# Low parts taken from GpSimd in the expert stages, and an earlier first chunk in two projections

## The chip, the cores and the metric

One core of one Trainium2 chip. The metric is the device time of one execution, in microseconds; the kernel before was timed in 3 runs.

## The reference

Two residual layers and a final RMSNorm over 1024 positions of 1024 values. Each layer normalises, projects, mixes tokens, projects out, and then runs an expert-choice mixture of experts. What matters here is the input projection and the experts:

```python
h = rmsnorm(x, norm_mix[i])
proj = h @ w_in                      # even: 1024 x 2816, odd: 1024 x 1184
...
# experts: 16, each takes its 128 best tokens
gates, idx = lax.top_k(aff.transpose(0, 2, 1), cap)
xs = h[idx]
g = xs @ w_gate                      # 1024 x 512 for each expert
u = xs @ w_up                        # 1024 x 512
y = (silu(g) * u) @ w_down           # 512 x 1024
out[idx] += y * gates
```

Everything is float32. The kernel keeps that precision by splitting each operand into a high part (rounded to the matmul's format) and a low part (the rest), and by adding three products: high by high, high by low, low by high.

## The kernel before, in words

The program is one order of work, written out by hand, for one core: even projection, dilated attention with a gMLP, output projection and routing, 16 experts, odd projection, dense attention, output projection and routing, 16 experts, final norm. Each engine runs its own instructions in that order, and waits only where data or a buffer is missing.

**The weight stream (class Stream, L163).** All weights of the program are one list of pieces of 128x1024 values (512 KB). `load` issues the next pieces on SyncE's queue (L202, L204) while there is a free slot for raw pieces; `conv` makes the high part on ScalarE (L225, or L235 with a gain) and then the low part, raw minus high, on VectorE (L232, or L236), and gives the raw slot back. With `pool=True` L232 goes to GpSimd (POOL) instead. The converted pieces lie in eight buffer pairs in the expert stages.

**The experts (out_moe).** For expert e the order on TensorE is: four pieces of "up" (`gate_up(e, "u", q)`, 6 matmuls of 128x512 each), with the first half of the next expert's tokens transposed after the second piece (`xsT`, L588); then the other half of these transposes, the 8 small matmuls of `index(e + 3)` (L572), four pieces of "gate" of expert e + 1, with the 4 transposes of `hT(e)` (L628) after the second; and four pieces of "down" (L644). VectorE makes `sg` = up times silu(gate) (L622), which `hT` transposes, and besides it the low parts `xl` and `tl` of the transposed operands (L149), the one-hot matrix of a later expert (L565) and the indices (L574, L576). GpSimd gathers the tokens (L578) and scatters the result (L659). After each piece `ahead(j)` (L593) converts the piece 7 places further on and issues loads. One piece in 12 has its low part made by POOL; that is the second "down" piece of expert e, which comes up after the third "up" piece of that expert, one for each of experts 0 to 14 in each layer. The output projection of layer 0 also gives low parts to POOL (four), in a call of its own.

**The projections (even_proj, odd_proj, class NormProj).** The tokens come in eight chunks of 128. `trans(c)` transposes chunk c on TensorE (8 transposes, L790), splits it in two halves (L148 on ScalarE, L149 on VectorE) and sums its squares (L793); `stat` turns these into 1/rms (13 tiny VectorE instructions in the even layer); `mm(c, j, n)` multiplies the chunk by four pieces, 8 steps of 3 matmuls (L259 to L261), two steps to a piece. In both projections chunks 0 and 1 are transposed before the first `mm`, and chunk c + 2 after `mm` of chunk c. In the even layer the queue of loads is: x chunk 0, weight pieces 0 and 1, x chunk 1, pieces 2 and 3, x chunks 2 and 3, further pieces as slots come free. In the odd layer the first four pieces are converted before the chunks of x can be read, since these wait for the last scatter of layer 0.

Of the kernel before, what the change touches and what calls it, by code (L numbers as in the profile page):

```python
# [257 lines left out]
def mm3(nc, out, ah, al, bh, bl, first, last):  # L258
    nc.tensor.matmul(out, ah, bh, start=first, stop=False)  # L259
    nc.tensor.matmul(out, ah, bl, start=False, stop=False)  # L260
    nc.tensor.matmul(out, al, bh, start=False, stop=last)  # L261
# [23 lines left out]
def out_moe(k, layer, stream, at, cva, n_a, n_early, n_late, mix, xload, xres, hd, out=None):  # L285
# [10 lines left out]
    with ExitStack() as ctx:  # L296
        ctx.enter_context(tc.manual_schedule())
        cvc = ctx.enter_context(tc.tile_pool(name=f"cvc{layer}", bufs=1, reuse_waits="tile")) if n_a < 4 else None
        base = at["out"]
# [6 lines left out]
        with lp, tk:  # L306
# [22 lines left out]
            g = k.gain(p2, i["norm_ffn"][layer], "gffn")  # L329
# [102 lines left out]
            for c in range(1, NCH):  # L432
# [3 lines left out]
                for s in range(16):  # L436
                    n, kk = divmod(s, 8)
# [30 lines left out]
            c = NCH - 1  # L468
# [56 lines left out]
            n = 64  # L525
# [62 lines left out]
                nc.tensor.transpose(pt[:, kk], d["xs"][:, c0:c0 + 128], k.ident)  # L588
            k.split(d["xh", q], d["xl", q], pt)

        AHEAD, EVERY = 7, 12

        def ahead(j):  # L593

            n = min(j + 1 + AHEAD, at["end"])
            while stream.n_conv < n:
                stream.conv(stream.n_conv + 1, pool=(stream.n_conv - at["g", 0]) % EVERY == 1, load=False)
            stream.load()

        def gate_up(e, nm, q):  # L600
# [166 lines left out]
class NormProj:  # L767
# [27 lines left out]
    def stat(self, c0, c1):  # L795
        self.k.rsqrt(self.p2, self.rstd[:, c0:c1], self.ss[:, c0:c1], EPS, 1.0 / DM, f"rs{c1 - c0}")

    def mm(self, c, j, n):

        nc = self.k.nc  # L800
        pt = self.pp.tile([128, 512], F32, name="pp")
        sl = slice(c * 128, (c + 1) * 128)
        for kk in range(NCH):
            bh, bl = self.stream.part(j + kk // 2, kk % 2, n)
            mm3(nc, pt[:, 0:n], self.hT[:, 0, kk, sl], self.hT[:, 1, kk, sl], bh, bl, kk == 0, kk == 7)
        return pt
# [27 lines left out]
def even_proj(k, stream, x_in, qk, vd, gd, first):  # L834

    tc, nc, i = k.tc, k.nc, k.i
    with ExitStack() as ctx:
        ctx.enter_context(tc.manual_schedule())  # L840
        p1 = ctx.enter_context(tc.tile_pool(name="ep1", bufs=1, reuse_waits="tile"))
        p2 = ctx.enter_context(tc.tile_pool(name="ep2", bufs=2, reuse_waits="tile"))
        cv = ctx.enter_context(tc.tile_pool(name="ecv", bufs=6, reuse_waits="tile"))
        ps = ctx.enter_context(tc.tile_pool(name="eps", bufs=2, space=PSUM, reuse_waits="tile"))
        pp = ctx.enter_context(tc.tile_pool(name="epp", bufs=3, space=PSUM, reuse_waits="tile"))
        gps = ctx.enter_context(tc.tile_pool(name="gps", bufs=2, space=PSUM, reuse_waits="tile"))
        stream.into((cv, 6))
        P = NormProj(k, stream, p1, p2, pp, ps)
        rq = p1.tile([128, NCH], F32, name="rq")
        z = p1.tile([128, NCH, 512], F32, name="z")  # L850
        von = p1.tile([128, 2, 8, 66], F32, name="von")
        k.consts(p1, "rac", "ras", nc.gpsimd)
        ra_c = k.c("rac").rearrange("p (c f) -> p c f", c=8)
        ra_s = k.c("ras").rearrange("p (c f) -> p c f", c=8)

        def stat(c0, c1):
            P.stat(c0, c1)
            nc.vector.tensor_scalar(rq[:, c0:c1], P.rstd[:, c0:c1], 0.125, None, op0=ALU.mult)

        def evac(kind, cols, c, pt):  # L860
            sl = slice(c * 128, (c + 1) * 128)
            if kind == "z":
                nc.scalar.activation(z[:, c], pt, AF.Gelu_apprx_tanh, scale=P.rstd[:, c:c + 1])
                return
            if kind == "v":
                (c0, n), = cols
                nh = n // 64
                h0 = (c0 - 1536) // 64
                ov = von[:, c % 2, 0:nh]
                nc.scalar.activation(ov[:, :, 0:64], pt[:, 0:n].rearrange("p (h d) -> p h d", d=64), AF.Copy,  # L870
                                     scale=P.rstd[:, c:c + 1])
                nc.gpsimd.dma_start(vd[sl, h0:h0 + nh], ov)
                return
            o = p2.tile([128, 512], F32, name="po", bufs=3)
            a = 0
            for c0, n in cols:
                nc.scalar.activation(o[:, a:a + n], pt[:, a:a + n], AF.Copy,
                                     scale=(rq if c0 < 768 else P.rstd)[:, c:c + 1])
                a += n
            ov = o.rearrange("p (h d) -> p h d", d=64)[:, :, 0:16]  # L880
            rope(nc, p2, ov, ov, ra_c[:, c, None, :].to_broadcast([128, 8, 8]),
                 ra_s[:, c, None, :].to_broadcast([128, 8, 8]), 8, "r")
            dst, a = (qk[1], 0) if len(cols) == 2 else (qk[0], 0 if kind == "q" else 512)
            nc.gpsimd.dma_start(dst[sl, a:a + 512], o)

        bg = []
        xs, gx = ExitStack(), ExitStack()
        P.xp = xs.enter_context(tc.tile_pool(name="exp", bufs=4, reuse_waits="tile"))

        def load(c):  # L890
            P.load(c, x_in[c * 128:(c + 1) * 128], nc.sync)
        load(0)
        stream.load(2)
        load(1)
        stream.load(4)
        load(2)
        load(3)
        P.trans(0)
        stream.conv(2)
        stat(0, 1)  # L900
        stream.conv(4)
        P.trans(1)
        stat(1, 2)
        nc.vector.memset(von[:, :, :, 64:66], 1.0)
        j = 0
        for gi, (kind, cols) in enumerate(EVEN_GROUPS):
            last = gi + 1 == len(EVEN_GROUPS)
            for c in range(NCH):
                if gi + 2 == len(EVEN_GROUPS) and c == 5:
                    gx.close()  # L910
                    bg = first(ps, cv)
                pt = P.mm(c, j, sum(n for _, n in cols))
                if gi == 0:
                    if c + 2 < NCH:
                        P.trans(c + 2)
                        stat(c + 2, c + 3)
                        if c + 4 < NCH:
                            load(c + 4)
                    if c == 2:
                        k.rest()  # L920
                    if c == 5:
                        xs.close()
                        gp = gx.enter_context(tc.tile_pool(name="gp1", bufs=1, reuse_waits="tile"))
                        bg = gmlp(k, z, gd, gp, gps)
                evac(kind, cols, c, pt)
                if not last and c in (1, 3, 6, 7):
                    if c == 7:
                        stream.drop(j, 4)
                    stream.conv(j + 4 + (1, 3, 6, 7).index(c) + 1)
                if gi and bg:  # L930
                    bg.pop(0)()
            j += 4
        stream.drop(j - 4, 4)
# [475 lines left out]
def odd_proj(k, stream, base, xin, cT, kp, krs, cdr, qd, kd, vdd, heads):  # L1409
# [4 lines left out]
    with ExitStack() as ctx:  # L1414
# [9 lines left out]
        P = NormProj(k, stream, p1, p2, pp, ps)  # L1424
# [3 lines left out]
        def load(c):  # L1428
            P.load(c, xin[c * 128:(c + 1) * 128], nc.sync if c < 3 else nc.scalar, DM if c else 512)
# [28 lines left out]
        def trans_c(c):  # L1458
            o = oc.pop(c)
            tp = ps.tile([128, 4, 128], F32, name="pt")  # L1460
            for j in range(3):
                nc.tensor.transpose(tp[:, j], o[:, j * 128:(j + 1) * 128], k.ident)
            sl = slice(c * 128, (c + 1) * 128)
            k.split(cT[:, 0, :, sl], cT[:, 1, :, sl], tp[:, 0:3])

        P.trans(0)
        P.stat(0, 1)
        P.trans(1)
        P.stat(1, 2)
        for c in range(NCH):  # L1470
            if c == 2:
                k.consts(p0, "rcc", "rds", nc.gpsimd)
            pt = P.mm(c, base, 416)
            if c + 2 < NCH:
                P.trans(c + 2)
                P.stat(c + 2, c + 3)
            if c + 3 < NCH:
                load(c + 3)
            if c > 1 and c % 2:
                for a in (c - 3, c - 2):  # L1480
                    trans_c(a)
            if c == 7:
                stream.conv(base + 8)
            evac_c(c, pt)
            if c % 2:
                norm_c(c - 1, c + 1)
            if c in (1, 3):
                stream.conv(base + {1: 5, 3: 6}[c])
# [67 lines left out]
        for part, j, n in (("q", base + 4, 512), ("k", base + 8, 256)):  # L1556
            tables(part)
            for c in range(NCH):
                pt = pts.pop(0) if pts else P.mm(c, j, n)
# [58 lines left out]
        def transpose4(dst, src):  # L1618
# [6 lines left out]
            else:  # L1625
                H.late.append(lambda: nc.scalar.activation(dst, cat(pt), AF.Copy))
        first = H.prep(0, transpose4)
        between = {(1, 0): [lambda: H.kr(0, None)], (1, 1): [lambda: H.kr(1, transpose4)] + first[2], (2, 0): first[3], (2, 1): first[4],
                   (3, 0): first[7], (3, 1): first[8]}
# [446 lines left out]
```

## Time and profile before

| what | value |
| --- | --- |
| runs | 2043.83, 2044.11, 2040.78 us; median 2043.83 |
| profiled execution | 2040.48 us, span 2038.7 us |
| TensorE busy | 1867.7 us (92%), granted clock 0.970 in the mean |
| VectorE busy | 1507.7 us (74%) |
| ScalarE busy | 1245.2 us (61%) |
| POOL busy | 504.1 us (25%) |
| low parts on VectorE, L232 into lo, raw from the ring | 243, mean 1416 ns |
| transfers | 384.78 MB, mean 189 GB/s |

Busy shares are means over stages with different limits, so the sections below go by stage. The expert stages run from about 655 to 962 us and from about 1690 to 2000 us of the span; the even projection starts with the span, the odd one at about 970 us. In the views, times are microseconds from the start of the span, a bracket holds the idle time ahead of an instruction and what ended it, and a group's time runs from the start of its first instruction to the end of its last.

### The profile page before, as it was taken

The page shows a single profiled execution, that of the slowest core. Times are in us where ns is not written, and L with a number is a line of the kernel's source. Part 1 is how long each engine was busy: PE and PEld are TensorE (multiplying, and loading weights), DVE is VectorE, ACT ScalarE, POOL GpSimd, SP SyncE. Part 2 cuts the span into 40 slices and gives each one's busy share as a digit, 9 for nine tenths or more (in the row PEclk, how much of TensorE's full clock was granted, in tenths as well). Part 3 has the DMA queues.
Part 4 walks back from the last instruction along what each step waited for, and adds up shares of the span by engine and source line. Part 5 has one row for each costly group of instructions (what it writes and reads, how often), then busy time and mean ns, then how long its engine had stood idle before and what let it go on. Part 6 is the DMA issues. An engine that isn't in the chain of part 4 may idle for free. (4 is left out here: it accounts for less than half of the span.)

```text
span 2038.7 us, 29998 instructions
## 1 busy us (share of the span) xinstructions
PE 1867.7 (92%) x10350; PEld 1563.4 (77%) x10350; DVE 1507.7 (74%) x3092; ACT 1245.2 (61%) x2020; POOL 504.1 (25%) x426
## 2 busy tenths in 40 slices
PE   8999999998995999998998799999998968999993
PEld 6888899997883777776887688888886846777772
DVE  5431246776557999997776688889995569999994
ACT  5322257775324777776634688889883326877783
POOL 0010100002102443541002243322212014444334
PEclk9999999999997999999899999999999979999996
DMA  6232355542555999994326554424115848999955
GB/s 228 71 104 78 128 138 136 128 122 85 207 208 181 378 384 373 373 385 95 124 78 209 95 75 87 69 45 54 37 30 163 305 169 311 384 372 387 375 183 196
DMA packets 214171, 384.78 MB, mean 189 GB/s; under 512 B 71937, under 2 KB 122881, under 8 KB 214018
## 3 DMA queue, kind: packets, MB, share of 16 engines
q1 hardware_dynamic: 190082, 303.43, 45.6%
q0 software_dynamic: 21200, 73.13, 12.0%
q10 hardware_dynamic: 2736, 6.29, 0.9%
q8 instruction: 82, 1.34, 0.3%
q14 instruction: 71, 0.58, 0.1%
HBM read 309.13 MB, written 66.32 MB: 184 GB/s over the span
## 5 line engine op out<-in xcount | busy, mean ns | idle before, releaser
L232 DVE TENSOR_TENSOR lo<-raw,hi 128x1024 fp32r<-128x1024 f32 x243 | 334.0, 1416 | 12.2 <-ACT hi L225 12.2
L225 ACT ACTIVATE hi<-raw 128x1024 fp32r<-128x1024 f32 x269 | 275.1, 1055 | 15.3 <-PE py L644 12.1
L259 PE MATMUL pp<-hi,hT 128*128 128x512 f32 (+2 forms) x576 | 213.2, 370 | 0.0
L260 PE MATMUL pp<-lo,hT 128*128 128x512 f32 (+2 forms) x576 | 211.6, 367 | 0.1
L261 PE MATMUL pp<-hi,hT 128*128 128x512 f32 (+2 forms) x576 | 211.2, 367 | 0.0
L1866 DVE TENSOR_REDUCE nm<-css 128x1 f32<-128x1024 f32 x128 | 156.0, 1219 | 41.3 <-PE css L1860 40.8
L149 DVE TENSOR_TENSOR PT<-cpt,PT 128x512 fp32r<-128x512 f32 x256 | 163.1, 678 | 4.3 <-ACT PT L148 1.9
L148 ACT ACTIVATE PT<-cpt 128x512 fp32r<-128x512 f32 x256 | 139.6, 597 | 40.4 <-PE cpt L1884 38.7
L1860 PE MATMUL css<-kT,qT 128*128 128x512 f32 x512 | 151.7, 398 | 10.8 <-ACT pe L1872 9.5
L1872 ACT ACTIVATE pe<-css,nm 128x1024 f32<-128x1024 f32 x128 | 143.8, 1123 | 11.6 <-DVE rinv L1892 7.7
L1884 PE MATMUL cpt<-csident,pe 128*128 128x128 f32 x1024 | 135.0, 274 | 1.1 <-DVE PT L149 0.8
L1884 PEld LDWEIGHTS cpt<-csident,pe 128*128 128x128 f32 x1024 | 116.8, 141 | 16.3 <-DVE PT L149 3.7
L261 PEld LDWEIGHTS pp<-hi,hT 128*128 128x128 f32 x576 | 109.4, 190 | 17.5
L260 PEld LDWEIGHTS pp<-lo,hT 128*128 128x128 f32 x576 | 109.5, 190 | 17.3 <-DVE lo L236 0.3
L259 PEld LDWEIGHTS pp<-hi,hT 128*128 128x128 f32 x576 | 109.7, 190 | 17.1
L1860 PEld LDWEIGHTS css<-kT,qT 128*128 128x128 f32 x512 | 96.0, 189 | 34.6 <-ACT pe L1872 10.9
L1902 PE MATMUL po<-PT,vv 128*128 128x512 f32 x256 | 112.4, 439 | 7.1 <-DVE o L1910 7.1
L1179 DVE CUSTOM_DVE_ANT_0 sm<-ass,csnat 128x256 f32<-128x256 f32 x176 | 67.4, 420 | 52.3 <-PE ass L1177 47.6
L1903 PE MATMUL po<-PT,vv 128*128 128x512 f32 x256 | 101.6, 397 | 0.0
L232 DVE TENSOR_TENSOR cT<-raw,cT 128x1024 fp32r<-128x1024 f32 x65 | 95.7, 1492 | 3.3 <-ACT cT L225 3.2
L578 POOL DMA_INDIRECT xs<-hd,idx x32 | 65.9, 2060 | 128.3 <-DVE gt L576 128.3
L1177 PE MATMUL ass<-kT,qT 128*128 128x256 f32 x384 | 96.4, 381 | 1.0 <-DMA kT<-kT 1.0
(447 smaller groups left out, 4819.5 us busy)
## 6 DMA issues: line engine op xcount, KB each, us to landing
raw<-in_moe_w_up_dram SPq DMA_DIRECT2D x112, 512.0 KB, 6.2
raw<-in_moe_w_down_dram SPq DMA_DIRECT2D x110, 512.0 KB, 6.2
raw<-in_moe_w_gate_dram SPq DMA_DIRECT2D x106, 512.0 KB, 6.5
attn<-in_moe_w_gate_dram SPq DMA_DIRECT2D x22, 512.0 KB, 6.5
attn<-in_moe_w_down_dram SPq DMA_DIRECT2D x18, 512.0 KB, 5.9
raw<-in_even_w_in_dram SPq DMA_DIRECT2D x16, 512.0 KB, 4.7
hd<-h POOLq DMA_DIRECT2D x16, 512.0 KB, 5.5
attn<-in_moe_w_up_dram SPq DMA_DIRECT2D x16, 512.0 KB, 6.5
```

What stands on the lines that cost most here:

```text
L148: self.nc.scalar.activation(hi, src, AF.Copy)
L149: (eng or self.nc.vector).tensor_tensor(lo, src, hi.bitcast(F32), op=ALU.subtract)
L225: nc.scalar.activation(hv, tv, AF.Copy)
L232: (nc.gpsimd if pool else nc.vector).tensor_tensor(lv, tv, hv.bitcast(F32), op=ALU.subtract)
L259: nc.tensor.matmul(out, ah, bh, start=first, stop=False)
L260: nc.tensor.matmul(out, ah, bl, start=False, stop=False)
L261: nc.tensor.matmul(out, al, bh, start=False, stop=last)
L1860: nc.tensor.matmul(ss[:, n], a[:, sl], m[:, n * 512:(n + 1) * 512], start=(j == 0), stop=(j == len(passes) - 1))
L1866: nc.vector.tensor_reduce(nm, B[b]["ss"], axis=AX.X, op=ALU.max, negate=True)
L1872: nc.scalar.activation(pe, B[b]["ss"], AF.Exp, bias=B[b]["nm"], accum_out=l)
L1884: nc.tensor.transpose(pt[:, kk], B[b]["pe"][:, kc * 128:(kc + 1) * 128], k.ident)
L1902: nc.tensor.matmul(po[g], vv[:, kc], PT[g][:, 0, kc], start=(kc == 0), stop=False)
```

## The change

POOL gets no low part in the experts: `ahead` converts with VectorE alone. In both projections the transposes of chunk 1 move from ahead of the first `mm` into it: in the even layer after 6 of its 8 steps, in the odd layer after 4. In the even layer weight pieces 2 and 3 are loaded ahead of x chunk 1, and all four pieces are converted before the statistics of chunk 0.

```diff
-        AHEAD, EVERY = 7, 12
+        AHEAD = 7
 
         def ahead(j):
             n = min(j + 1 + AHEAD, at["end"])
-            while stream.n_conv < n:
-                stream.conv(stream.n_conv + 1, pool=(stream.n_conv - at["g", 0]) % EVERY == 1, load=False)
+            stream.conv(n, load=False)
             stream.load()
...
-    def mm(self, c, j, n):
+    def mm(self, c, j, n, between=None):
...
         for kk in range(NCH):
+            if between and kk == between[0]:
+                between[1]()
             bh, bl = self.stream.part(j + kk // 2, kk % 2, n)
...
         load(0)
-        stream.load(2)
+        stream.load(4)
         load(1)
-        stream.load(4)
         load(2)
         load(3)
         P.trans(0)
-        stream.conv(2)
+        stream.conv(4)
         stat(0, 1)
-        stream.conv(4)
-        P.trans(1)
-        stat(1, 2)
...
-                pt = P.mm(c, j, sum(n for _, n in cols))
+                pt = P.mm(c, j, sum(n for _, n in cols), (6, lambda: P.trans(1)) if gi == 0 and c == 0 else None)
                 if gi == 0:
+                    if c == 0:
+                        stat(1, 2)
                     if c + 2 < NCH:
...
         P.trans(0)
         P.stat(0, 1)
-        P.trans(1)
-        P.stat(1, 2)
...
-            pt = P.mm(c, base, 416)
+            pt = P.mm(c, base, 416, None if c else (4, lambda: P.trans(1)))
+            if c == 0:
+                P.stat(1, 2)
```

## Rows read from the trace of the kernel before

**Rows 1.** Waits of TensorE over the whole span: us in total, times, longest.

```profile
PE tp L628 <- DVE sg L622: 26.8, 28, 1.8
```

**Rows 2.** Windows: length, busy us of each engine, granted clock, DMA share, GB/s.

```profile
700.00:750.00 50.00, 47.25 (x241) 37.96 (x240) 48.84 (x48) 38.29 (x45) 25.68 (x9) 1.00 1.03 373
912.00:930.00 18.00, 18.00 (x85) 14.59 (x84) 16.57 (x16) 15.03 (x18) 3.98 (x2) 1.00 0.61 204
975.00:980.00 5.00, 4.58 (x17) 4.46 (x18) 4.03 (x21) 2.79 (x6) 0.00 (x0) 0.52 0.76 271
```

**Rows 3.** Timeline of POOL in the experts of layer 0: start, us, instruction.

```profile
756.92 4.83 POOL L659 DMA_INDIRECT xa<-y,idx  x1 [7.72 <-PE pu L261]
761.22 2.97 POOL L232 TENSOR_TENSOR lo<-attn,hi 128x1024 fp32r<-128x1024 f32 x1
...
912.67 1.59 POOL L659 DMA_INDIRECT xa<-y,idx  x1 [7.73 <-PE pu L261]
916.19 2.40 POOL L232 TENSOR_TENSOR lo<-attn,hi 128x1024 fp32r<-128x1024 f32 x1 [1.93 <-ACT hi L225]
930.78 1.57 POOL L659 DMA_INDIRECT xa<-y,idx  x1 [12.20 <-PE pu L261]
```

**Rows 4.** Timeline of VectorE in the experts of layer 0.

```profile
761.28 4.00 DVE L232 TENSOR_TENSOR lo<-attn,hi 128x1024 fp32r<-128x1024 f32 x1 [0.40 <-ACT hi L225]
765.20 0.68 DVE L622 TENSOR_TENSOR sg<-pu,sg 128x512 f32<-128x512 f32 x1
...
769.47 4.61 DVE L232 TENSOR_TENSOR lo<-raw,hi 128x1024 fp32r<-128x1024 f32 x4
774.01 1.21 DVE L565 TENSOR_TENSOR oh<-csslots,slot 128x1024 bf16<-128x1024 f32 x1
...
917.03 2.64 DVE L232 TENSOR_TENSOR lo<-attn,hi 128x1024 fp32r<-128x1024 f32 x1 [0.69 <-ACT hi L225]
```

**Rows 5.** Timeline of TensorE in the experts of layer 0.

```profile
668.51 0.66 PE L628 MATMUL tp<-csident,sg 128*128 128x128 f32 x4 [1.76 <-DVE sg L622]
...
764.60 0.40 PE L261 MATMUL pg<-hi,xl 128*128 128x512 f32 x1
765.93 0.66 PE L628 MATMUL tp<-csident,sg 128*128 128x128 f32 x4 [0.93 <-DVE sg L622]
```

**Rows 6.** Last expert load of layer 0 issued (SyncE's queue), last low part (VectorE).

```profile
910.39 0.33 SPq L204 DMA_DIRECT2D raw<-in_moe_w_down_dram  x1
...
949.61 1.22 DVE L232 TENSOR_TENSOR lo<-raw,hi 128x1024 fp32r<-128x1024 f32 x1 [0.94 <-ACT hi L225]
```

**Rows 7.** Timeline of all engines at the start of the even projection.

```profile
9.26 2.74 DVE L236 SCALAR_TENSOR_TENSOR lo<-raw,gains,hi 128x512 fp32r<-128x512 f32 x4 [0.95 <-ACT hi L235]
...
11.79 1.94 PE L790 MATMUL pt<-csident,xin 128*128 128x128 f32 x8 [4.84 <-DMA xin<-in_x_dram]
...
12.91 2.70 ACT L235 ACTIVATE hi<-raw,gains 128x512 fp32r<-128x512 f32 x4 [1.85 <-DMA raw<-in_even_w_in_dram]
...
13.38 0.78 PE L259 MATMUL pp<-hi,hT 128*128 128x512 f32 x1
...
17.30 0.39 PE L259 MATMUL pp<-hi,hT 128*128 128x512 f32 x1
...
20.82 1.03 PE L790 MATMUL pt<-csident,xin 128*128 128x128 f32 x8
```

**Rows 8.** Timeline of all engines at the start of the odd projection.

```profile
971.78 2.12 PE L790 MATMUL pt<-csident,xin 128*128 128x128 f32 x8 [10.74 <-DMA xin<-xa]
...
974.56 0.69 DVE L149 TENSOR_TENSOR hT<-pt,hT 128x512 fp32r<-128x512 f32 x1 [0.26 <-ACT hT L148]
...
975.42 1.97 PE L790 MATMUL pt<-csident,xin 128*128 128x128 f32 x8 [1.53 <-DMA xin<-xa]
...
979.88 0.35 PE L261 MATMUL pp<-hi,hT 128*128 128x416 f32 x1
...
982.90 1.04 PE L790 MATMUL pt<-csident,xin 128*128 128x128 f32 x8
```

## The prediction

> **What bounds the kernel now.** I read the windows first. In an expert stage TensorE is busy 47.25 of 50 us and VectorE 48.84 of 50 [rows 2]: both are nearly full, so the question is which waits for which. The waits of TensorE answer it: the transposes of `sg` wait for VectorE's product in 28 places, 26.8 us together [rows 1]. Two layers have 32 such places; in the rest nothing is lost.
>
> The timelines say why VectorE is late. Take the expert around 760 us. POOL starts its low part at 761.22 and needs 2.97 us, to 764.19. VectorE starts its own low part at 761.28 and ends at 765.28, 4.00 us, where four of the same kind in a row take 4.61 us, 1.21 for the first and 1.13 for each further one [rows 3, 4]. So the VectorE instruction ends one normal duration after POOL's end: it stood still while POOL ran. The same pair late in the layer agrees: POOL 916.19 to 918.59, VectorE 917.03 to 919.67, 1.08 after POOL [rows 3, 4]. The product follows at 765.20, takes 0.68, and TensorE starts the transposes at 765.93, 0.05 later [rows 4, 5]. The matmul before them started at 764.60, and matmuls of this kind follow each other at 0.23 us (the window of 912 to 930 us has 72 of them and 12 transposes in 18.00 busy us, so about 0.23 each [rows 2]). Without the wait the transposes start at 764.83: 1.10 us are lost per expert.
>
> The bound of an expert is therefore: TensorE's own work, plus 1.10 us put in by one POOL instruction through VectorE. Where POOL's low part ends early enough, no wait is left: the late expert takes 930.78 - 912.67 = 18.11 us, the one of 756.92 one eighth of 912.67 - 756.92 = 155.75, that is 19.47 (eight scatters lie in between) [rows 3]. The difference, 1.36, is an upper bound of the loss, since the late experts also do without the one-hot matrix and the index.
>
> **Part 1, POOL's low parts (15 in each layer).** VectorE gets one more low part per expert, 1.13 us, and its long one shrinks from 4.00 to 1.21. Its load per expert is then 12 x 1.13 for low parts, 1.13 to 1.21 for the one-hot matrix, four operations like `sg` at 0.60 to 0.68, and two tiny ones, an estimate of 0.2: 13.6 + 1.2 + 2.6 + 0.2 = 17.6 us. TensorE's load is 19.47 - 1.10 = 18.37. VectorE has 0.8 us to spare: TensorE becomes the bound. Is `sg` in time at its place in the queue? Ahead of it stand now two low parts instead of a long one. Even if both start only at 761.28, they end at 763.6, the product at 764.3, before 764.83. So the cost of the added instruction is nothing as long as these 0.5 us hold; if the two low parts started 1.5 us later, the whole wait would be back.
>
> Sum: experts 1 to 12 of each layer lose 1.10 each, 13.2. Expert 0 waits longer: 1.76 of idle time by the bracket [rows 5], and VectorE comes late there with four low parts in a row, so I count 1.4 of it and leave 0.4. Experts 13 and 14 lose nothing now, and 15 has no POOL low part. 14.6 per layer; the row of waits, taken over both layers, shows the same pattern twice (26.8 / 28 = 0.96 of idle time, to which the restart adds about 0.15) [rows 1]. **29.2 us**; by the bound of 1.36 per expert it would be 35, by the idle time alone (0.9 each) 24.
>
> What is late next? Loads. An expert moves 19.47 us x 373 GB/s = 7.26 MB [rows 2], and in 18.37 us that is 395 GB/s. No row shows such a mean. But the last expert load was issued at 910.39, and the last low part started at 949.61 [rows 6]: loads are issued 39 us before they are used. Were 373 GB/s a ceiling, each expert would lose 1.10 us of this lead, 14 us over 13 experts, and 25 would be left. So I cost it at nothing. SyncE's queue is only helped: raw slots that waited for POOL come free earlier, in the same order. POOL's own queue, gathers and scatters, loses a neighbour and gains no wait.
>
> The Trainium skill speaks against this: "DMA: Bandwidth & Descriptors", section "Where 436 GB/s comes from", puts HBM to SBUF at about 358 GB/s per core. By that rule an expert's 7.26 MB need 20.3 us, more than it takes now, and no gain would be left. The window shows 373 GB/s over 50 us [rows 2], so here the measurement decides against the figure.
>
> **Part 2, even projection.** Now TensorE waits 4.84 us for x chunk 1, transposes it from 11.79, starts the first matmul at 13.38 and the next transposes at 20.82 [rows 7]. Afterwards the first matmul needs only chunk 0 and the first converted half piece: its high part is there when VectorE begins the low part at 9.26 [rows 7], so about 9.3; the low part follows at 10.0. The work up to the next transposes is the same, 24 matmuls and 8 transposes, and takes 20.82 - 11.79 = 9.03 now, of which the first 5.5 at the lower clock: the matmul at 13.38 takes 0.78, the one at 17.30 0.39. Moved as it is, with 0.3 for the first low part, it ends at 18.6, 2.2 earlier. The weights keep up: piece 2 takes the place of x chunk 1 in the queue (landed 11.79), piece 3 that of piece 2 (12.91), x chunk 1 comes two pieces after, at 12.91 + 1.12 = 14.0, while TensorE reaches its transposes at 15.7 to 17.4. ScalarE and VectorE convert eight half pieces before the split of chunk 1, at 2.70 to 2.74 for four [rows 7], done by about 15.2. What follows is that the transposes of chunk 2 need the PSUM buffers that chunk 1 frees only now: two splits, about 1.4 us after the transposes, just covered by the last 6 matmuls. Bounds: if the clock rises at 17.3 as before, all but the last steps run slow and 0.9 remains; if chunk 1 lands 4 us late, -1; if all ran at the upper clock, 24 x 0.23 and 1.03 would be over as the last converted piece allows, near 17: 3.8. I take **2.0**, near the stretch moved as it is, since the rows hold that stretch. The tail of the stage follows: TensorE has no other idle time until the attention, so the shift is kept.
>
> **Part 3, odd projection.** TensorE transposes chunk 0 at 971.78, ends at 973.90, waits for chunk 1 until 975.42, and reaches chunk 2 at 982.90 [rows 8]. Then steps 0 to 3 go into the gap: they need the first half of chunk 0, while the second low half starts at 974.56 [rows 8], so they start at about 974.0 at the slow clock (416 columns of 512, so 0.19 us a matmul at the upper clock and about 0.37 at the lower). The stretch from 975.42 to 982.90 holds the same 8 transposes and 24 matmuls; moved as it is, 7.48 from 974.0, it ends at 981.5: 1.4 earlier. If the clock rises where it does now (the mean granted clock of 975 to 980 is 0.52, the lower level of 1.2 GHz [rows 2], and the matmul at 979.88 is already short [rows 8]), 0.9; all at the upper clock, 974.0 + 24 x 0.19 + 1.04 = 979.6, 3.3. The trace has no row for a clock after a shorter pause; I take **1.5**, at the stretch as it is. A loss would need the split of chunk 1 to come late: its transposes end at about 979.3, three us before chunk 1 is multiplied.
>
> **Sum.** 29.2 + 2.0 + 1.5 = 32.7. The profiled execution took 2040.48 (span 2038.7 and 1.8 around it), which gives 2007.8; from the median of the runs, 2043.83, it is 2011.1. I predict 2010.
>
> **The rivals.**
> - A, forecast: all steps as above. With 24 to 35 for part 1 and 1.8 to 4.9 or so for the rest (7.1 if both starts ran at the upper clock), between runs of 2040.8 and 2044.1: 2002 to 2018. Chance 0.70.
> - B, the starts give nothing (a late chunk 1, an unchanged clock): 2014. For it: the clock's rise is not something the order of work alone sets. Chance 0.08.
> - C, VectorE stays late: its 0.8 us of slack are spent by waits for ScalarE (a bracket of 0.40 and one of 0.69 stand in [rows 4]), and half of the wait returns: 14.6 + 3.5, 2026. Against: the late experts had VectorE waiting for ScalarE and TensorE with no idle time [rows 2]. Chance 0.08.
> - D, loads set the pace: decided when the lead of 39 us shrinks by more than the 14 worked out, say since scatters and loads disturb each other more; the later half of each layer then runs at 19.47: 2026. Chance 0.06.
> - E, no change in the experts: loads hold the period of 19.47 from the first expert on, and only the starts give their 3.5: 2040. It decides if the lead of 39 us is not there when a layer begins. Chance 0.03. The rule cited in part 1 would give this case.
> - F, slower: the long VectorE instruction is not POOL's low part but its scatter, which is being issued from 756.92 for 4.83 us [rows 3]. Then 2.79 stays and 1.13 is added for each of 26 experts: 2043.8 + 29 - 3.5 = 2069. It decides if the long one stays at 4.00 without a low part on POOL. Against: in the late pair the scatter took 1.59 and was over at 914.26, yet VectorE's low part took 2.64 [rows 3, 4]. Chance 0.05.
>
> A measurement of this kernel can tell 0.2%, 4 us. Faster: A to D, 0.92; within 0.2%: E, 0.03; slower: F, 0.05. The range reaches from 2003 over A and B into C and D, to 2025.
>
> **What would show it.** In the profile after: no POOL low parts in the experts, VectorE's low parts at 1.2 us without a long one, scatters 18.3 to 18.4 us apart in the middle of a layer, and waits of the transposes for `sg` in some 4 places instead of 28. In the even layer a first matmul at 9.3 and the transposes of chunk 2 at 18 to 19; in the odd layer a first matmul some 2 us after the first transposes instead of after those of chunk 1. Wrong would be: a VectorE low part of 4 us left (F), ScalarE waiting for raw pieces (D), or TensorE's wait moved to another operand of VectorE (C).

## The result and the profile after

The changed kernel takes 2009.1 us (median of 4 runs, 2004.95 to 2016.94) beside 2043.0 for the kernel before on the same chip: ratio 0.984, 95% interval 0.9807 to 0.9873, 33.9 us less. On another chip, later, it was 2006.1 (5 runs) beside 2037.6: 0.9847, interval 0.9829 to 0.9865. The forecast was 2010.0, by a sum of 32.7.

The profiled execution is the slowest of those runs (span 2014.4). The steps of the change stand in it clearly; a later part of this text says where else it lost time.

Waits of TensorE in the changed kernel (us in total, times, longest). The wait for `sg` has gone from 28 places to 4 [rows 1]; other waits, outside the experts, now lead the list:

```profile
PE po L1901 <- DVE o L1909: 16.7, 8, 9.7
...
PE apP L1349 <- DVE attn L1258: 7.6, 1, 7.6
...
PE tp L627 <- DVE sg L621: 2.1, 4, 0.8
```

The windows of the changed kernel, with the columns of [rows 2]. TensorE is busy 50.00 of 50 us in the expert stage instead of 47.25, VectorE is a little less full, and all transfers together move 385 GB/s instead of 373:

```profile
700.00:750.00 50.00, 50.00 (x254) 40.98 (x253) 48.03 (x54) 41.02 (x46) 9.02 (x5) 1.00 1.03 385
912.00:930.00 18.00, 18.00 (x86) 14.69 (x85) 16.33 (x17) 15.14 (x17) 1.57 (x1) 1.00 0.44 115
```

One expert of the changed kernel, all engines, answering to [rows 3 to 5]. POOL has no low part left. VectorE's low parts come in twos of 2.35 us, none of them longer than 1.23. `sg` ends at 776.35 and the transposes begin at 777.75 without a bracket: TensorE arrives there 1.4 us after VectorE has finished. The scatters (POOL) are 18.32 us apart:

```profile
769.82 1.83 POOL L658 DMA_INDIRECT xa<-y,idx  x1 [9.02 <-ACT y L654]
...
773.40 2.35 DVE L232 TENSOR_TENSOR lo<-raw,hi 128x1024 fp32r<-128x1024 f32 x2
...
775.66 0.69 DVE L621 TENSOR_TENSOR sg<-pu,sg 128x512 f32<-128x512 f32 x1
...
777.75 0.60 PE L627 MATMUL tp<-csident,sg 128*128 128x128 f32 x4
...
788.14 1.84 POOL L658 DMA_INDIRECT xa<-y,idx  x1 [9.02 <-ACT y L654]
```

The starts of both projections on TensorE, answering to [rows 7, 8]. In the even layer the first matmul stands at 9.21; the transposes of chunk 1 lie between matmuls at 16.30, those of chunk 2 at 18.58 instead of 20.82. In the odd layer matmuls start 2.25 us after the first transposes, and from there to the transposes of chunk 2 are 8.26 us instead of 11.12:

```profile
9.21 0.80 PE L259 MATMUL pp<-hi,hT 128*128 128x512 f32 x1 [2.33 <-ACT hi L235]
...
14.86 0.44 PE L259 MATMUL pp<-hi,hT 128*128 128x512 f32 x1
...
16.30 1.03 PE L789 MATMUL pt<-csident,xin 128*128 128x128 f32 x8
...
18.58 1.11 PE L789 MATMUL pt<-csident,xin 128*128 128x128 f32 x8
...
956.99 1.11 PE L789 MATMUL pt<-csident,xin 128*128 128x128 f32 x4 [10.48 <-DMA xin<-xa]
958.50 1.09 PE L789 MATMUL pt<-csident,xin 128*128 128x128 f32 x4 [0.40 <-DMA xin<-xa]
959.24 0.70 PE L259 MATMUL pp<-hi,hT 128*128 128x416 f32 x1
...
960.43 0.36 PE L259 MATMUL pp<-hi,hT 128*128 128x416 f32 x1
...
965.25 1.04 PE L789 MATMUL pt<-csident,xin 128*128 128x128 f32 x8
```

The time by stages, from the timelines. A stage ends with the event named; "again" is a second profile of the changed kernel, on the other chip.

| stage, up to | before | after | after, again |
|---|---|---|---|
| first score matmul, even layer | 273.0 | 270.9 | 270.7 |
| end of the even attention (last `apP`) | 228.9 | 231.1 | 229.0 |
| last scatter of layer 0 | 460.6 | 446.1 | 445.0 |
| first score matmul, odd layer | 164.7 | 162.3 | 160.4 |
| last `po` matmul, odd layer | 416.1 | 428.7 | 422.6 |
| end | 495.3 | 475.3 | 475.4 |
| span | 2038.7 | 2014.4 | 2003.0 |

The stages that the change touches (lines 1, 3, 4, 6) are shorter in both profiles, by 39 and 42 us together; lines 2 and 5, the two attentions, where nothing was changed, are 15 and 7 longer. A good part of that is a shift: the mark of line 5 lies where the attention passes into the output projection, and when it comes late, line 6 is shorter. Lines 5 and 6 together are 911.4, 904.0 and 898.0 us, that is 7.4 and 13.4 less, where the experts of layer 1 give 15.0 by their own rows. So nearly 8 us are lost there in the first profile, and 1.6 in the second.

### The profile page after: what moved, and what is told of

Its sections match the earlier page's. It is cut to its first block, busy times and chain, and to the rows that moved or that the text cites. A ratio compares the mean times of both kernels' runs of the same rounds, so it can differ in the third digit from the quotient of the medians.

```text
span 2014.4 us, 29972 instructions
## 1 busy us (share of the span) xinstructions
PE 1866.7 (93%) x10350; PEld 1570.2 (78%) x10350; DVE 1467.7 (73%) x3122; ACT 1245.2 (62%) x2020; POOL 367.9 (18%) x396
## 5 line engine op out<-in xcount | busy, mean ns | idle before, releaser
L232 DVE TENSOR_TENSOR lo<-raw,hi 128x1024 fp32r<-128x1024 f32 x260 | 310.0, 1226 | 23.2 <-ACT hi L225 23.0
L578 POOL DMA_INDIRECT xs<-hd,idx x32 | 70.3, 2195 | 197.1 <-DVE gt L576 197.1
L259 PE MATMUL pp<-hi,aTh 128*128 128x512 f32 x208 | 87.5, 421 | 0.4 <-DVE o L1212 0.4
```

The costliest lines, as they stand in the source:

```text
L232: (nc.gpsimd if pool else nc.vector).tensor_tensor(lv, tv, hv.bitcast(F32), op=ALU.subtract)
```

## The experiments

The theory before them: a two-input operation of POOL and a two-input operation of VectorE, all operands in SBUF, do not run beside each other; one stands still until the other's whole instruction is over. The kernel before let this happen once per expert, just ahead of `sg`. Rivals: the scatter holds VectorE; any POOL work does; the loads set the pace.

**Each part alone.** e1 is the kernel before with only this edit (the later experiments leave it in or undo it):

```
-        AHEAD, EVERY = 7, 12
+        AHEAD = 7
...
-            while stream.n_conv < n:
-                stream.conv(stream.n_conv + 1, pool=(stream.n_conv - at["g", 0]) % EVERY == 1, load=False)
+            stream.conv(n, load=False)
```

> The kernel before with the experts' low parts on VectorE alone; the projections as before. Theory (POOL's low part holds VectorE, and VectorE holds TensorE): scatters 18.33 to 18.4 us apart, as with the whole change, some 30 us off the experts, 2043 - 30 = 2013 us. Rival (the two starts carry part of the gain beyond their own 4 to 5 us, because an earlier stage changes what loads meet): fewer than 25 us, over 2018.

Measured: 2009.89 beside 2038.33, ratio 0.9864 (0.9849 to 0.9879), 28.4 us less. In the first twelve steps from expert to expert of layer 0 the transposes of `sg` are 18.32 to 18.38 us apart, as in the whole change, instead of 19.46 to 19.54. So part 1 does alone what it does in the sum.

e2 is the changed kernel with that edit undone: the new starts, and the low parts on POOL.

> The changed kernel with POOL's low parts put back. Theory: scatters 19.47 apart again; the chunk 2 transposes of the even layer at 18.6 us instead of 20.8 (2.2 earlier), and in the odd layer 6.1 us instead of 7.5 from the first matmul stretch to chunk 2 or better; together 4 to 5 us, 2038.5 us. Rival (the starts are swallowed by the next wait, since the attention waits for transfers): time within 1 us of before, 2042.

Measured: 2035.43 (11 runs), ratio 0.9987 (0.9978 to 0.9996): 2.9 us less, the interval 0.8 to 4.5; 4 to 5 were expected. The transposes of chunk 2 start at 19.13 in the even layer, where 18.6 was expected. The wait for `sg` is back, 26.9 us in 28 places. Part by part the two give 28.4 + 2.9 = 31.3, where the whole gives 31 to 34: nothing shows that they help or hinder each other.

**Is it the low part, or its place?** e3 is the changed kernel with POOL's low parts back, but on another piece of the expert:

```
-            stream.conv(n, load=False)
+            while stream.n_conv < n:
+                stream.conv(stream.n_conv + 1, pool=(stream.n_conv - at["g", 0]) % EVERY == 8, load=False)
```

> The changed kernel, but one low part in 12 on POOL again, another one: it comes up after the second down piece, ahead of the one-hot matrix, and not just ahead of the product that TensorE waits for. Theory (each POOL low part costs VectorE 2.8 us standing still and saves it 1.1, wherever it stands, so VectorE needs 19.0 us of an expert): scatters 19.0 to 19.4 apart, 2025 to 2036 us. Rival (only the place ahead of the product hurts): scatters 18.3 to 18.5 apart, 2008 to 2014 us.

Measured: 2009.6, ratio 0.9852 (0.9836 to 0.9867): no slower than without POOL's low parts. My form of the theory, that such a low part costs its time wherever it stands, fell. Timeline of e3, VectorE and POOL, and one of its windows, with the columns of [rows 2]:

```profile
742.82 3.47 DVE L232 TENSOR_TENSOR lo<-raw,hi 128x1024 fp32r<-128x1024 f32 x3
745.72 5.14 POOL L232 TENSOR_TENSOR lo<-raw,hi 128x1024 fp32r<-128x1024 f32 x1 [2.57 <-issue]
746.22 1.21 DVE L565 TENSOR_TENSOR oh<-csslots,slot 128x1024 bf16<-128x1024 f32 x1
747.36 4.57 DVE L232 TENSOR_TENSOR lo<-raw,hi 128x1024 fp32r<-128x1024 f32 x2
...
757.00 0.68 DVE L622 TENSOR_TENSOR sg<-pu,sg 128x512 f32<-128x512 f32 x1
...
700.00:750.00 50.00, 50.00 (x252) 40.96 (x251) 49.84 (x51) 41.62 (x47) 24.03 (x8) 1.00 1.03 386
```

POOL's low part, 2.40 us alone [rows 3], takes 5.14 here: POOL is held first, by VectorE's one-hot matrix and low part, and then holds VectorE (4.57 for two low parts that take 2.35 elsewhere, so 2.2 lost). But `sg` comes nine microseconds later and is in time: the wait of its transposes is 1.6 us in two places. VectorE paid out of its idle time: it is busy 49.84 of 50 us here, 48.03 in the changed kernel, and TensorE 50.00 in both. What cost time before was the place. From the first to the last transposes of `sg` e3 needs 272.3 and 272.8 us in the two layers, 0.6 to 0.7 more than the changed kernel, so almost no slack is left.

**Twice the cost, and POOL work without reads.** e4 is the changed kernel in which POOL computes, into scratch, the low part that VectorE has just made, on the piece that POOL had before; it takes one late raw slot less for space. This work is extra.

```
+                if extra is not None:
+                    nc.gpsimd.tensor_tensor(extra..., tv, hv.bitcast(F32), op=ALU.subtract)
```

> The changed kernel, and POOL makes the low part of one piece in 12 a second time, into a tile that nobody reads (VectorE makes all of them too; two raw slots fewer in all). POOL's place is that of the kernel before. Theory (hold): one VectorE instruction per expert takes 4 us again, VectorE needs 17.6 + 2.8 = 20.4 us, scatters 20.1 to 20.5 apart: 13 x 2 x 1.9 us over the changed kernel, some 2055 to 2062. Rival (the saved 1.1 us of VectorE or the scatter was the matter): 18.4 apart, 2010 us.

Measured: 2070.71, ratio 1.0151 (1.0136 to 1.0167), more than the 2055 to 2062 expected, in the direction expected. e4, the timeline of POOL, VectorE and TensorE in one expert:

```profile
740.03 4.82 POOL L662 DMA_INDIRECT xa<-y,idx  x1 [7.72 <-ACT y L658]
...
743.93 5.60 DVE L232 TENSOR_TENSOR lo<-raw,hi 128x1024 fp32r<-128x1024 f32 x2
744.33 2.97 POOL L234 TENSOR_TENSOR scr<-raw,hi 128x1024 fp32r<-128x1024 f32 x1
749.45 0.68 DVE L625 TENSOR_TENSOR sg<-pu,sg 128x512 f32<-128x512 f32 x1
...
750.18 0.66 PE L631 MATMUL tp<-csident,sg 128*128 128x128 f32 x4 [2.07 <-DVE sg L625]
```

VectorE's two low parts end at 749.53, two normal durations after POOL's end at 747.30: both ended behind it, in 5.60 us instead of 2.35, and `sg` waits behind them; the transposes of `sg` lose 52.1 us in 32 places and stand 20.6 us apart. Twice the work ahead of `sg` on VectorE and the same hold: that is the pattern of the kernel before, by itself, with the low part on VectorE as well.

e5 gives POOL three operations of the same shape in each expert that only write (`nc.gpsimd.memset(extra, 0.0)`, three times).

> The changed kernel, and per expert three POOL memsets of 128x1024 into a tile that nobody reads (two raw slots fewer in all): POOL writes SBUF for about as long as a low part takes, but reads nothing. Theory in the form that the hold comes of reading the same memory side: VectorE's instructions stay at 1.2 us, scatters 18.3 to 18.4 apart, 2005 to 2015 us. Rival (any POOL work beside VectorE holds it): a VectorE instruction of 2 to 4 us per expert, scatters 19 to 20.4 apart, 2030 to 2060.

Measured: 2003.91, ratio 0.9825 (0.9807 to 0.9843). The timeline of e5 shows POOL's writes and VectorE's low parts over each other, both at their usual length:

```profile
770.60 2.36 DVE L232 TENSOR_TENSOR lo<-raw,hi 128x1024 fp32r<-128x1024 f32 x2 [0.32 <-ACT hi L225]
771.17 3.57 POOL L235 MEMSET scr<- 128x1024 f32 x3
773.48 2.35 DVE L232 TENSOR_TENSOR lo<-attn,hi 128x1024 fp32r<-128x1024 f32 x2
```

So not any POOL work holds VectorE: of the two kinds tried, the one that reads SBUF does, and the one that only writes does not. The Trainium skill states it so ("SBUF — State Buffer", section "SBUF: two separate sides"): the pair of ports that the two engines share goes whole to the one that starts first, for its whole instruction, and a VectorE operation with two SBUF inputs meets it only against a GpSimd operation that reads SBUF. e3 (either engine waits, each time until an instruction of the other has ended) and e5 (no wait against writes) agree. Who started first cannot be read from the profile: in e4 the low part of VectorE begins at 743.93, 0.40 us ahead of POOL's, and is still the one that stands still.

**Do loads limit?** e6 is the changed kernel with fewer early and late raw slots, so that expert loads are issued closer to their use:

```
-        out_moe(k, 0, stream, at, cva, 4, 8, 4, ...
+        out_moe(k, 0, stream, at, cva, 4, 2, 1, ...
...
-        out_moe(k, 1, stream, at, cva, 3, 15, 5, ...
+        out_moe(k, 1, stream, at, cva, 3, 6, 1, ...
```

> The changed kernel with 9 raw slots fewer in the experts of layer 0 and 13 fewer in those of layer 1. Theory (TensorE is the bound, loads keep up at 395 GB/s): scatters still 18.33 to 18.4 apart, 2004 to 2014 us, no ScalarE wait for raw pieces. Rival (loads are at their ceiling of some 385 GB/s, and the lead of 24 pieces hid it): in the second half of the experts scatters go to 18.8 to 19.5 and ScalarE waits for raw pieces; 2015 to 2030.

Measured: 2003.86, ratio 0.9823 (0.9803 to 0.9842), no change; the experts stay 18.32 us apart up to the thirteenth. The last expert load of layer 0 and the last low part of e6 (SyncE's queue, VectorE), answering to [rows 6]:

```profile
913.28 0.33 SPq L204 DMA_DIRECT2D attn<-in_moe_w_down_dram  x1
...
931.42 1.23 DVE L232 TENSOR_TENSOR lo<-attn,hi 128x1024 fp32r<-128x1024 f32 x1 [1.12 <-ACT hi L225]
```

The lead is 18 us, where the changed kernel has 33 (the last four issued from 898.11 on, the last low part at 935.06) and the kernel before 39. Half of it is enough.

The loads are now the nearest limit, though. These are waits of SyncE's queue between 700 and 900 us, ahead of issuing loads (us in total, times, longest), first of the kernel before, then of the changed kernel:

```profile
SPq L202 <- DVE lo L232: 69.8, 70, 2.1
...
SPq L202 <- DMA raw<-in_moe_w_gate_dram: 29.6, 21, 3.1
SPq L202 <- DVE lo L232: 27.1, 32, 2.1
```

Before, the queue waited for low parts, which give the raw slots back (111 us for VectorE's and 35 for POOL's, over L202 and L204). In the changed kernel it waits 114 us for earlier loads and 37 for low parts. From issue to the start of the high part on ScalarE the lead falls from 38 us in the middle of layer 0 to 31 at its end, in e6 from 25 to 16, while the kernel before holds 39 almost to the end. So the loads run a little slower than the experts now use them, and the lead covers it until the layer is over.

**The rest of POOL's low parts.** e7 takes them from the output projection of layer 0 as well, the one place where the change left them:

```
-            stream.conv(base + (4 if layer else 8), pool=layer == 0, load=False)
+            stream.conv(base + (4 if layer else 8), load=False)
```

> The changed kernel, and the four low parts that POOL makes ahead of the output projection of layer 0 go to VectorE too. In the changed kernel TensorE waits 7.6 us there for a chain of small VectorE instructions, three of which stand still beside POOL for 2.1 each. Theory (same hold): the three shrink to 0.2 to 0.7, VectorE gets 4.5 of low parts, the wait falls from 7.6 to 3 to 4: 3 to 5 us off, 2005 us in the median. Rival (the four low parts now stand ahead of the chain and cost as much): no change, 2009.

Measured: 1999.66, ratio 0.9813 (0.9797 to 0.9829). Once more, beside the changed kernel:

> The kernel of e7 once more (the output projection of layer 0 without low parts on POOL), beside the changed kernel on one chip. Theory: it is 3 to 5 us faster than the changed kernel, the wait for `attn` being 3.3 instead of 7.6 us. Rival: the 9 us between it and the changed kernel's first measurement lie in the chip, and on one chip the two differ by less than 2 us.

Measured: 2000.82 beside 2006.12 for the changed kernel on the same chip, 5.3 us less; the ratios to before are 0.9813 (0.9793 to 0.9833) and 0.9847 (0.9829 to 0.9865). The stage itself ends 4.2 to 5.2 us earlier (223.8 and 224.8 us against 229.0; the other profiles with POOL's low parts there have 227.7 to 231.2). The cause stands in the timeline of the changed kernel, POOL and VectorE in that stage:

```profile
489.28 7.05 POOL L232 TENSOR_TENSOR lo<-raw,hi 128x1024 fp32r<-128x1024 f32 x3 [23.06 <-ACT hi L225]
...
491.74 2.31 DVE L1230 TENSOR_TENSOR dd<-o,o 128x8 f32<-128x8 f32 x1 [1.86 <-DMA o<-o2d]
494.08 2.27 DVE L1231 TENSOR_TENSOR mm<-dd,o 128x8 f32<-128x8 f32 x1
...
498.33 2.83 DVE L1254 TENSOR_TENSOR attn<-o,ww 128x512 f32<-128x512 f32 x1
```

and in that of e7, the same three:

```profile
488.79 0.17 DVE L1230 TENSOR_TENSOR dd<-o,o 128x8 f32<-128x8 f32 x1
...
490.01 0.17 DVE L1231 TENSOR_TENSOR mm<-dd,o 128x8 f32<-128x8 f32 x1
...
493.00 0.68 DVE L1254 TENSOR_TENSOR attn<-o,ww 128x512 f32<-128x512 f32 x1
```

Two operations on 8 columns take 0.17 us each, and 2.3 when they meet a low part on POOL; the chain to `attn` is 6.4 us longer by them and by the third, and TensorE's wait for `attn` falls from 7.6 to 3.3 or 3.4 without. This version is faster than both kernels.

**The order of the loads.** e8 is the changed kernel with the even projection's loads in the old order (x chunk 1 ahead of the second weight piece).

> The changed kernel with the loads of the even layer in the order of before: x chunk 1 ahead of weight pieces 2 and 3. Theory (the work is what was moved, the order of loads is worth little): pieces 2 and 3 come 1 us later, still before step 4 at 14.9 us, chunk 2's transposes at 18.6 to 18.8 as in the changed kernel. Rival (the order carries the gain): TensorE waits for piece 2 or 3, chunk 2's transposes at 19.5 or later.

Measured, in one run: 2004.24. Its transposes of chunk 2, on TensorE:

```profile
19.40 1.25 PE L789 MATMUL pt<-csident,xin 128*128 128x128 f32 x8 [0.86 <-DVE hT L149]
```

19.40, between the two expectations and nearer to the rival's, with a wait of 0.86 for the split of a chunk that the changed kernel does not have. The order matters by about that wait; the time of one run cannot show it.

**The loss in the odd attention.** In the changed kernel TensorE waits 9.72 and 9.30 us for `o` in the two profiles, 2.48 before.

> The changed kernel itself, on the chip of e7 and e9. Theory: its undisturbed time lies near 2004, between 2003 and 2007, since its experts and the two starts give 34.7 us by their own rows, and only some executions lose more in the attention stages, which the change does not touch. Rival: it stays at 2008 to 2010, and something in the attention stages is later in every execution by 4 to 6 us because of the change.

Measured: 2006.12 (2004.83 to 2009.4), its median by the theory. But the profile of it has the wait too.

e9 is e7 with one more buffer for `o` and one less for `ol`, which takes away that VectorE's `o` waits for the DMA that reads the old one:

```
-            ol = pol.tile([64, 512], F32, name="ol")
+            ol = pol.tile([64, 512], F32, name="ol", bufs=1)
...
-            o = pol.tile([64, 512], F32, name="o")
+            o = pol.tile([64, 512], F32, name="o", bufs=3)
```

> The changed kernel with two edits: the output projection of layer 0 makes all its low parts on VectorE (as in e7), and in the odd attention the normalised tile `o` gets three buffers while `ol` keeps one. Theory: what the changed kernel loses behind its own gain are waits of TensorE for `o` in the odd attention (16.7 us in 8 places in its trace, 9.72 in one of them, where VectorE's `o` waits for the DMA that reads the buffer's old contents) and for `attn` in the output projection (7.6 us). With a third buffer the wait of `o` for that DMA goes: 4 to 9 us less than e7 alone if the waits come in most executions, that is 1991 to 1996. Rival: the long wait stands in some executions only, and `o` is late because of what stands ahead of it on VectorE (the quotient waits for POOL, and POOL for its own load); then TensorE keeps waiting 7 us or more for `o` and the time stays within 2 us of e7, 1998 to 2002.

Measured: 2000.71 beside 2000.82 for e7: no gain, against the theory; the wait is 5.06 us. The first profile of the changed kernel does show VectorE's `o` waiting for that DMA, in two places:

```profile
1409.80 0.68 DVE L1909 TENSOR_TENSOR o<-po,ol 64x512 f32<-64x512 f32 x1 [3.04 <-DMA oda<-o]
...
1528.17 0.69 DVE L149 TENSOR_TENSOR aTl<-aT,aTh 128x512 fp32r<-128x512 f32 x1 [5.54 <-ACT aTh L148]
...
1533.25 0.68 DVE L1909 TENSOR_TENSOR o<-po,ol 64x512 f32<-64x512 f32 x1 [3.19 <-DMA odb<-o]
```

The second profile, and both of e7, have no such wait ahead of TensorE's long one, so e9 had nothing to gain there: the buffer is a part of the first profile's loss and not of the wait that they share. The timeline of the second profile of the changed kernel, SyncE's queue, ScalarE, VectorE and TensorE:

```profile
1505.22 0.36 SPq L1969 DMA_DIRECT2D aT<-oda  x1
...
1518.35 0.63 ACT L148 ACTIVATE aTh<-aT 128x512 fp32r<-128x512 f32 x1 [8.58 <-DMA aT<-oda]
1519.01 0.69 DVE L149 TENSOR_TENSOR aTl<-aT,aTh 128x512 fp32r<-128x512 f32 x1 [8.40 <-ACT aTh L148]
...
1520.82 0.67 DVE L1909 TENSOR_TENSOR o<-po,ol 64x512 f32<-64x512 f32 x1
...
1521.54 0.80 PE L1901 MATMUL po<-PT,vv 128*128 128x512 f32 x1 [9.30 <-DVE o L1909]
```

`o` is queued behind the low part of `aT`, the first piece of the output projection, and that waits for a load. From issue to ScalarE's start this load takes 13.1 us here, 10.3 in the first profile, 9.3 in the second of e7, 6.0 in e8, 5.1 in e1, 4.8 before. The wait for `o` follows it: 9.3, 9.7 (3.2 of it for the buffer), 5.5, 2.2, 1.5, 2.5 us. Of the eleven profiles with the new starts nine have a load of 8.9 to 13.4 us and two, e3 and e8, of 5.3 and 6.0; the two with the old starts have 4.8 and 5.1. So the change does not make it long in every execution; whether it makes that likelier, two profiles of the old starts cannot show. Why the load takes 5 us in one execution and 13 in another stays open too.

The wait costs less than its length. From the first score matmul of the odd layer to the first transposes of `sg` in layer 1 it is 582.7 us in e1 (wait 1.5), 582.8 in e6 (5.7), 585.0 in e5 (9.6) and 585.0 in the second profile (9.3): up to six us cost nothing, nine cost about 2. After the long wait the output projection lacks small waits that TensorE has there otherwise: from the last `po` matmul to its own last matmul it is 111.8 us in e1 and 107.7 in the second profile. The first profile needs 590.9. It loses 4.5 of that around 1410 us, by the first of its two waits for the buffer and a granted clock of 0.50 (the lower level, 1.2 GHz) from 1412 to 1414 behind it; no other profile waits there.

## Why the prediction was right, point by point

**Part 1, 29.2: right, measured 28.4 alone and about 30 by the trace.** From the first to the last transposes of `sg` it is 285.3 and 285.6 us in the two layers before, 271.6 and 272.2 after: 13.7 and 13.4, where the experts 1 to 12 were to give 13.2 per layer. The loss per expert was 19.48 - 18.35 = 1.13, predicted 1.10. Expert 0 gave about 1.4, as predicted: from the first matmul of the routing's ranking (L549) to its `sg` transposes 30.1 us became 28.7 in layer 0. VectorE's new low part cost nothing, as worked out; the margin ahead of the transposes is 1.4 us, more than the 0.5 that I left as a bound, because the two low parts also start earlier.

**What was late next: nothing, but the loads are close.** All transfers went to 384 to 397 GB/s in windows of 50 us, and the lead shrank from 39 to 33 us, not to 25. E and D are out by the rows and by e6: TensorE has no idle time in the middle of a layer, and ScalarE's ten gaps of 0.3 us ahead of a raw piece, D's sign, are no longer than those beside them that end on TensorE. SyncE's queue waits for the loads, as D has it, but the layer ends before the lead does.

My reading of the windows against the page was wrong: 373 and 385 GB/s hold gathers and scatters besides the loads. The queue of the loads alone moved 15.97 MB in the 50 us of the kernel before and 16.07 in those of the changed one, 319 and 321 GB/s. Over 707 to 720 us of the changed kernel it is 4.86 MB, 374 GB/s. The figure of the Trainium skill's page "DMA: Bandwidth & Descriptors", section "Where 436 GB/s comes from", about 358 GB/s for HBM to SBUF, is exceeded only by this shorter row; the windows of 50 us do not decide against it.

C is out: 4 waits for `sg`, as predicted. F, the scatter, is out by its own condition: the scatters are still there, the first of layer 0 at 4.87 us even without a low part on POOL, and no VectorE low part of the experts is longer than 1.23. In e3 VectorE is held at 747 us, when no scatter runs (the next begins at 751.01).

**Part 2, 2.0: right.** First matmul at 9.21 (predicted 9.3), transposes of chunk 2 at 18.58 (18.6). They come 2.24 earlier; the first score matmul comes 2.1 to 2.4 earlier, 1.7 in e2. How much is gained depends on when the granted clock rises from the lower level to the upper. Short matmuls begin at 14.86 in the changed kernel, at 15.92 in e2, at 17.30 before. e1, with the old start, ran its first stage 1.0 us shorter than before: that much two executions of the same order differ.

**Part 3, 1.5: the mechanism right, the size too small.** From the first transposes to those of chunk 2 the gain is 2.9 us in the changed kernel and 2.0 in e2 (970.24 to 979.39). The term was mis-sized at the place of the clock's rise to the upper level: I let the stretch run as it did, mostly at the lower level, but here the short matmuls begin 3.4 us after the first transposes (960.43 after 956.99) and not 8.1 (979.88 after 971.78). Where TensorE waits less among the transposes ahead of its first matmul, the rise comes earlier (a wait of 0.40 us and a rise after 3.4 here, 0.86 and 4.9 in e2, 1.53 and 8.1 before); my bound, all at the upper clock, was 3.3. Over all kernels with the new starts, the stretch from the last scatter to the first score matmul of the odd layer is 160.2 to 164.5 us, with the old ones 163.6 and 164.7: the gain is there in most executions, not in each.

**The end of the sum: right by a little luck.** Against 32.7 stand 15.1 and 15.0 for the experts, 2.2 and 2.4 for the starts, together 34.7, while the runs give 31 to 34. From the first score matmul of the odd layer to the first transposes of `sg` in layer 1 it is 581.1 to 590.9 us over the 13 profiles, a spread that is more than both starts are worth, and I had no term for it. What decides there (a load that lands late, waits for a buffer, the granted clock) was not among the rivals. The lower end of rival A is a slip: by its own terms, 35 and 4.9 off a run of 2040.8, it is 2001 and not 2002.

**A finer point that fell.** In the expectation of e3 I argued from VectorE's load that a held low part costs its time. e3 shows that it costs only where the operation behind it has no time to spare. What carried the forecast was the reading of the place (the row of waits, the low part just ahead of `sg`), not the load.

## What to carry to other kernels

An operation that an off-path engine does "for free" may hold the engine that feeds the critical one: look in the timeline for an instruction that is longer than its siblings and ends one normal duration after an instruction of another engine. Then ask what is queued behind it, since a held instruction costs only if the next one is wanted at once; moving it to where there is slack (e3) gave the same as removing it. Two operations of 0.17 us took 2.3 each beside POOL, so small operations on a chain are the worst neighbours.

## What the runs showed that I had not expected

- The hold goes both ways, and POOL is the one that starves: beside back-to-back VectorE operations a POOL low part of 2.40 us took up to 6.55 (e3).
- Most scatters ahead of POOL's low part show 4.83 us on POOL [rows 3], 4.82 again in e4 at the same place, 2.39 in e3, and 1.83 in the changed kernel, where no low part follows. But the first scatter of each layer shows 4.87 and 4.83 there too, and in the kernel before one with a low part behind it shows 1.59 (at 912.67). What POOL does in those 3 us no row shows.
- In the even attention TensorE waits about 1.0 us for a DMA (`kT`) at the same place in all 13 profiles. Behind it the granted clock stayed at 1.00 in four (e1, e3, e6, the first of e7) and fell to 0.50, the lower level, in nine: longest in e5 and in the first profile of the changed kernel, which has 0.50 from 290 to 298 us, where the kernel before has 0.79. That is most of the 2.2 us that this stage lost in that profile; the second profile lost 0.1.
